# One more place for raw and one for split weights, and two query chunks interleaved between the layers of a two-layer encoder

## Chip, cores, metric

One Trainium2 chip, of which the kernel uses one core. The metric is the device time of one execution in microseconds (us); lower is better. TensorE is PE in the profile (its weight loads are PEld), VectorE is DVE, ScalarE is ACT, GpSimd is POOL, and SyncE is SP, on whose queue all transfers of weights are issued.

## The reference, cut to what matters

Two requests (256 and 512 tokens, each with 16 meta tokens in front, 800 rows in all) go through two layers. All is fp32.

```python
for i in range(2):
    mix = mla_mixer(h) if i == 0 else gqa_mixer(h)       # dense latent attention; windowed, grouped, with sinks
    h = layer_norm(ALPHA * h + mix, ln1_g[i], ln1_b[i])
    h = layer_norm(ALPHA * h + sqrelu_mlp(h, w1[i], w2[i]), ln2_g[i], ln2_b[i])

def sqrelu_mlp(x, w1, w2):                               # 1024 -> 4096 -> 1024
    h = relu(x @ w1)
    return (h * h) @ w2

def gqa_mixer(x):                                        # first steps of it
    qkv = x @ w_qkv                                      # 16 query heads, 4 key and 4 value heads of 64
    q, k = partial_rope(q), partial_rope(k)              # cos and sin on the first 16 of each 64
```

## The kernel before, in words

**Number format and weights.** Every fp32 operand of a large product is split in two fp32r parts, hi (a cast on ACT) and lo (value minus hi, on DVE), and each product is three matmuls (`mm3`, L426 to L428). A weight tile therefore passes through two places: SP loads 512 KB into a raw tile (`wraw`), ACT casts it into the hi half of a split tile (`wsp`), and DVE subtracts for the lo half (L587 and L589 in the attention parts, L1239 and L1245 in the MLP parts). There are three raw places and three split places, used in turn; a raw place is free again when both halves are made, a split place when its last matmul is done.

**Order.** Inside each of four parts (attention 0, MLP 0, attention 1, MLP 1) a `Plan` lists the tasks. PE keeps the order in which tasks are written. For ACT, DVE, POOL and SP a planner with costs per task and a number of places per kind of tile (the dictionary that begins `"wsp": 3, "wraw": 3`) chooses the order, and the program is issued in that order. Every engine then runs its own list strictly in order.

**The MLP parts.** Hidden chunks are made in pairs (`up_pair`) and multiplied down in groups of four (`down_group`), both by a scheme with 7 products instead of 8. POOL adds raw weights together first (L1258), and ACT and DVE split the sums. In a down group the seven products use weights called 1, 7, 6, 5, 3, 2, 4 in this order; products 1, 6, 5 and 3 all accumulate in the same banks X, and after each of them DVE adds the banks into `acc` (L1552) before PE may write them again. In layer 1 a product is 18 matmuls of 512 columns over three banks.

**The seam between the layers.** `attention1()` begins with the last 1/8 of layer 0's down product (`down`, 16 steps of 12 matmuls, half 0 of the tokens first; each step's bank is added to `acc` at L1803, and the sums for the mean run over POOL and DVE at L1807 and L1810 in `ssb`). Then come the second layer norm of layer 0 and the projections of layer 1. The norm of a half has three PE tasks: `mean` (a matmul with 1/1024, L603), `sums` (L618) and `scale` (L628). After `mean` DVE subtracts (L606), ACT squares (L608), DVE and POOL add squares (L612); after `scale` DVE multiplies (L633), ACT applies gain and bias (L636) and casts hi (L575), DVE makes lo (L577). The results `hb` are the right operands of the projections: query chunks `rope("q", c, half, w)` of four steps with two `hb` tiles each (6 matmuls a step), then values (four of 24 matmuls for half 0), then chunks 2 to 7. A finished query chunk is rotated by DVE (L1847, L1850), POOL (L1852) and DVE (L1855). In PE's order the norm of half 0 stands inside the down steps of half 1 (mean after step 0, sums after step 4, scale after step 6). The norm of half 1 has its mean between query chunks 0 and 1, its sums after the first step of chunk 2, its scale two steps later.

Of the kernel before, what the change touches and what calls it, by code (L numbers as in the profile page):

```python
# [12 lines left out]
F32 = mybir.dt.float32  # L13
# [341 lines left out]
def tile_encoder(ctx: ExitStack, tc: tile.TileContext, ins: dict, y):  # L355
# [64 lines left out]
        for key in [("up", j) for j in UP_FIRST[:2]] + [("dn", 7, i) for i in range(3)]:  # L420
            use(key, None, where="given")
    use(("dn", 7, 3), ins["w2c_1"][3], where="held")
    W = Weights(nc, wp, specs, 3, 3, 2)

    def mm3(out, lh, ll, rh, rl, start, stop, **kw):
        nc.tensor.matmul(out, lh, rh, start=start, stop=False, **kw)  # L426
# [64 lines left out]
    with ExitStack() as st:  # L491
        xp = pool("xp", side="right", stack=st)
        x = [xp.tile([P, 8, NT], F32R, tag=f"x{i}", name=f"x{i}") for i in range(2)]
        cos0 = xp.tile([P, NT], F32, tag="cos0", name="cos0")
        sin0 = xp.tile([P, NT], F32, tag="sin0", name="sin0")
        slices = []
        for _ in range(3):
            W.load(4)
            slices.append(W.parts)
        for k in range(8):  # L500
            xr = xp.tile([P, NT], F32, tag="xr", name=f"xr{k}", bufs=5)
            if k % 2 == 0:
                slices[0][k // 2]()
            for c in [slice(0, HALF), slice(HALF, NT)] if k < 2 else [slice(0, NT)]:
                nc.sync.dma_start(xr[:, c], ins["xT0"][k][:, c])
                split(x[0][:, k, c], x[1][:, k, c], xr[:, c])
            if k % 2 == 0:
                slices[1][k // 2]()
                slices[2][k // 2]()
        nc.sync.dma_start(gb, ins["ln_gb"])  # L510
        nc.sync.dma_start(grms, ins["rms_g"])
        nc.sync.dma_start(cos0, ins["rope0"][0])
        nc.sync.dma_start(sin0, ins["rope0"][1])
        craw = xp.tile([P, 2, NT], F32, tag="craw", name="craw")
        ss = [ssq, xp.tile([P, NT], F32, tag="ss", name="ss")]
        for o in IN_ORDER:
            w = W.get(("in", o))
            for h in range(2):
                c = slice(h * HALF, (h + 1) * HALF)
                ps = ps_w(f"in{o}{h}")  # L520
                gemm(ps[:, :HALF], w, 8, P, 0, x, (h * HALF, (h + 1) * HALF))
                pv = ps[:, :HALF]
                if o == 8:
                    sh = xp.tile([P, HALF], F32, tag="ksh", name=f"ksh{h}", bufs=2)
                    V.tensor_tensor(kr[:, h], pv, cos0[:, c], ALU.mult)
                    V.stream_shuffle(sh, pv, SWAP16)
                    V.tensor_tensor(sh, sh, sin0[:, c], ALU.mult)
                    V.tensor_tensor(kr[:, h], kr[:, h], sh, ALU.add)
                    continue
                which, first = (0, o == 0) if o < 6 else (1, o == 6)  # L530
                if o < 6:

                    g = grms[:, o : o + 1]
                    S.mul(cq[0][:, o, c], pv, g)
                    V.scalar_tensor_tensor(cq[1][:, o, c], pv, g, cq[0].bitcast(F32)[:, o, c], ALU.mult, ALU.subtract)
                else:
                    S.copy(craw[:, o - 6, c], pv)
                if first:
                    S.activation(ss[which][:, c], pv, AF.Square)
                else:  # L540
                    sq = xp.tile([P, HALF], F32, tag="sq", name=f"sq{o}{h}", bufs=2)
                    S.activation(sq, pv, AF.Square)
                    V.tensor_tensor(ss[which][:, c], ss[which][:, c], sq, ALU.add)
            if o == 7:
                for h in range(2):
                    c = slice(h * HALF, (h + 1) * HALF)
                    rs = rstd_bcast(xp, [ss[1][:, c]], HALF, 256, eps_rms, f"kv{h}")
                    for i in range(2):
                        r = craw[:, i, c]
                        V.scalar_tensor_tensor(r, r, grms[:, 6 + i : 7 + i], rs, ALU.mult, ALU.mult)  # L550
                        split(ckv[0][:, i, c], ckv[1][:, i, c], r)
# [6 lines left out]
        return [(x, y) for x in names for y in ("hi", "lo")]  # L558


    WSP = []

    def spare(given):

        return lambda k: [x for x in WSP if all(x is not y for y in given)][k]
# [1 line left out]
    def steps(plan):  # L567
# [13 lines left out]
        def weights(src, nm, tag="wsp", make=None):  # L581

            w = src.shape[-1]
            r = new("wraw", lambda: wp.tile([P, 1024], F32, tag="wraw", name=f"wraw{nm}", bufs=3))
            d = new(tag, make)
            plan.task("SP", 3.6 * w, lambda: nc.sync.dma_start(r.t[:, :w], src), writes=[r], new=[r])
            plan.task("ACT", ACT(w), lambda: S.copy(d.t[:, 0, :w], r.t[:, :w]), reads=[r], writes=[(d, "hi")], new=[d])  # L587
# [85 lines left out]

    SEQ = {0: (272, 0, 2, [(0, 272)]), 1: (528, 272, 4, [(0, 264), (264, 528)])}
    wo, l0 = ExitStack(), ExitStack()
    WSP.extend([w] + [W.get((x, 0), 0) for x in ("qr", "kv")])
    a0 = {}

    def open_output():
# [15 lines left out]

    def attention0():
        plan = Plan(
            {"wsp": 3, "wraw": 3, "w": 4, "s": 2, "qy": 2, "qsh": 2, "v0": 2, "v1": 2, "nm": 6, "rs": 6, "p": PROBS, "pt": 2, "ptm": 2, "sqa": 6, "xr": 3},
            {
                "wsp": lambda k: WSP[k],  # L700
                "w": lambda k: ps_w(f"wa_{k}"),
# [478 lines left out]
    def mlp_middle(mp, sqp, late_sum, T, n, l, tiles, yt=None):  # L1180


        plan = Plan(
            {"wsp": 3, "wraw": 3, "wx": 1, "w22": 1, "h2": 14, "sq": 6, "w": 8},
            {
                "h2": lambda k: h2_tile(mp, f"{l}_{k}", n),
                "sq": lambda k: sq_tile(sqp, f"{l}_{k}"),
# [19 lines left out]
        def raw(src, nm, tag="wraw"):  # L1207

            w = src.shape[-1]
            if tag == "wraw":  # L1210
                r = new(tag, lambda: wp.tile([P, 1024], F32, tag="wraw", name=f"wraw{nm}", bufs=3))
            else:
                r = new(tag, lambda: mp.tile([P, 1024], F32, tag=tag, name=f"{tag}{nm}", bufs=1))
            plan.task("SP", 3.6 * w, lambda: nc.sync.dma_start(r.t[:, :w], src), writes=[(r, 0), (r, 1)], new=[r])
            return r
# [552 lines left out]

    def attention1():
        plan = Plan(  # L1770
            {"wsp": 3, "wraw": 3, "wh": 1, "w": 8, "sqb": 6, "ssb": 1, "ssc": 1, "sqc": 6, "rt": 2, "sh": 1, "sma": 4, "smb": 3, "pta": 2, "ptb": 2,
             "rm": 4, "nm": 4, "rs": 4, "es": 4, "pk": 4, "ptm": 2, "mask": 1},
            {
                "wsp": spare([x for _, x in W.ready.values()]),
# [289 lines left out]
        for hf in range(2):  # L2064
            for x, t in enumerate((cos1, sin1)):
                plan.task("SP", 1400, lambda x=x, t=t, hf=hf: nc.sync.dma_start(t[hf], ins["rope1"][x][:, hf * HALF : (hf + 1) * HALF]), writes=[("rope", x, hf)])
        after0 = {0: mean0, 4: sums0, 6: scale0}
        for o in range(8):
            down(0, o)
        for o in range(8):  # L2070
            down(1, o)
            if o in after0:
                after0[o]()
        for c in range(2):
            w = wq(c)
            for i, f in enumerate(rope("q", c, 0, w)):
                f()
                if (c, i) == (0, 3):
                    mean1()
        wv = [weights(ins["w_v"][i], f"v{i}") for i in range(2)]  # L2080
        for f in values(0, wv):
            f()
        for c in range(2, 8):
            w = wq(c)
            for i, f in enumerate(rope("q", c, 0, w)):
# [256 lines left out]
```

## Time and profile before

| | us |
|---|---|
| median of 3 runs | 1798.51 (1796.97 to 1799.83) |
| the profiled execution, own time | 1798.46 |
| its span in the trace | 1796.4 |
| PE busy | 1757.5 (98%) |
| PE weight loads busy | 1626.9 (91%) |
| DVE busy | 1363.0 (76%) |
| ACT busy | 1017.1 (57%) |
| POOL busy | 639.1 (36%) |

The span is the time between the first and the last instruction that the profiler saw; the execution's own time has 2.1 us around it. A matmul's record is longer than its share of the engine, since matmuls overlap: a 384-column matmul lasts 0.34 us and the next one starts 0.175 us after it. So where PE counts as fully busy it may still be late; the distance from start to start tells. In a row of the timeline the bracket gives the idle time before the instruction and what ended it.

### The profile page before, as it was taken

What the parts mean: (1) busy time and instruction counts of PE and PEld (TensorE: products, weight loads), DVE (VectorE), ACT (ScalarE), POOL (GpSimd) and SP (SyncE); (2) the same over time, 40 slices, a digit from 0 to 9 for tenths busy, and PEclk for the clock granted to TensorE, in tenths of its full rate; (3) what the DMA queues carried; (4) which work ended last, traced back from release to release, by engine and by line L of the source; (5) the groups of instructions that cost most, each with busy time, mean ns of one, the idle gap of its engine ahead of it and who ended that gap; (6) DMA issues with size and microseconds to landing.
All of it is one profiled execution on the core that took longest, in us unless ns stands there. A gap on an engine that the chain in (4) does not pass through costs nothing.

```text
span 1796.4 us, 28830 instructions
## 1 busy us (share of the span) xinstructions
PE 1757.5 (98%) x10808; PEld 1626.9 (91%) x10808; DVE 1363.0 (76%) x2641; ACT 1017.1 (57%) x2141; POOL 639.1 (36%) x529
## 2 busy tenths in 40 slices
PE   9999999999999999999999999999999999999997
PEld 9988988889999999999999898778989888988995
DVE  5498888876876787778776777876875787778777
ACT  5377777774655445545553527775665446544652
POOL 0011111112245445545533133232244556556623
PEclk9999999999999999999999999999999999999998
DMA  5110001104311211222122121111311221222122
GB/s 198 54 36 23 27 22 38 34 29 142 113 59 47 87 58 56 83 71 71 59 94 89 51 101 48 32 40 64 114 59 47 71 71 59 83 71 71 58 84 94
DMA packets 38444, 121.70 MB, mean 68 GB/s; under 512 B 4640, under 2 KB 9376, under 8 KB 38176
## 3 DMA queue, kind: packets, MB, share of 16 engines
q1 hardware_dynamic: 38304, 119.85, 20.1%
q8 instruction: 85, 1.39, 0.3%
q14 instruction: 55, 0.45, 0.1%
HBM read 116.69 MB, written 3.15 MB: 67 GB/s over the span
## 4 chain that ended last, share of the span: by engine, by line
PE 79%; DVE 11%; ACT 4%; issue 3%; POOL 2%; DMA 1%; SPq 0%; DVEq 0%; ACTq 0%; POOLq 0%
PE w L426 14%; PE w L427 13%; PE w L428 13%; PE wb L426 4%; PE wb L427 4%; PE wb L428 4%; DVE wsp L1245 3%; PE wa L426 2%; PE wa L428 2%; PE wa L427 2%; PE wa L978 2%; DVE h L1287 2%; PE sa L426 2%; PE wb L2018 1%; PE in L427 1%
## 5 line engine op out<-in xcount | busy, mean ns | idle before, releaser
L426 PE MATMUL w<-h,wsp 128*128 128x400 f32 x632 | 218.3, 345 | 1.8 <-DVE acc L1552 1.1
L427 PE MATMUL w<-h,wsp 128*128 128x400 f32 x632 | 218.3, 345 | 0.0
L428 PE MATMUL w<-h,wsp 128*128 128x400 f32 x632 | 217.5, 344 | 0.1
L1552 DVE TENSOR_TENSOR acc<-acc,w 128x400 f32<-128x400 f32 (+1 forms) x306 | 176.8, 615 | 21.9 <-PE w L428 19.6
L1287 DVE TENSOR_TENSOR h<-sq,h 128x384 fp32r<-128x384 f32 (+1 forms) x165 | 138.0, 852 | 23.1 <-ACT h L1285 23.1
L914 POOL TENSOR_TENSOR p<-p,rs 106x512 f32<-106x512 f32 (+1 forms) x40 | 42.6, 1066 | 264.9 <-ACT pt L953 77.5
L426 PE MATMUL w<-wsp,h 128*128 128x512 f32 x300 | 119.4, 398 | 5.5 <-DVE acc L1552 5.5
L426 PEld LDWEIGHTS w<-h,wsp 128*128 128x128 f32 x632 | 118.8, 188 | 4.4 <-DVE acc L1552 3.0
L428 PEld LDWEIGHTS w<-h,wsp 128*128 128x128 f32 x632 | 118.7, 188 | 1.0 <-DVE wsp L1245 0.7
L428 PE MATMUL w<-wsp,h 128*128 128x512 f32 x300 | 119.2, 397 | 0.4
L427 PEld LDWEIGHTS w<-h,wsp 128*128 128x128 f32 x632 | 118.6, 188 | 0.9 <-DVE h L1287 0.5
L427 PE MATMUL w<-wsp,h 128*128 128x512 f32 x300 | 118.9, 396 | 0.0
L428 PE MATMUL w<-t,wsp 128*128 128x400 f32 (+1 forms) x336 | 114.5, 341 | 0.0
L427 PE MATMUL w<-t,wsp 128*128 128x400 f32 (+1 forms) x336 | 114.1, 340 | 0.0
L426 PE MATMUL w<-t,wsp 128*128 128x400 f32 (+1 forms) x336 | 114.0, 339 | 0.0
L1293 POOL TENSOR_TENSOR sq<-sq,sq 128x400 f32<-128x400 f32 (+1 forms) x56 | 75.1, 1341 | 70.2 <-DVE h L1287 61.9
L1285 ACT CAST h<-sq 128x384 fp32r<-128x384 f32 (+1 forms) x165 | 84.4, 518 | 26.1 <-POOL sq L1293 24.3
L1466 DVE TENSOR_TENSOR sq<-sq,w 128x400 f32<-128x400 f32 (+1 forms) x69 | 38.6, 560 | 60.5 <-PE w L428 60.1
L1258 POOL TENSOR_TENSOR wraw0d<-wraw0d,wraw0d 128x512 f32<-128x512 f32 x48 | 69.2, 1461 | 42.8 <-DMA wraw0d<-in_w2b_dram 29.5
L427 PE MATMUL w<-hc,wsp 128*128 128x384 f32 x232 | 78.8, 340 | 0.5 <-DVE hc L1372 0.3
L426 PE MATMUL w<-hc,wsp 128*128 128x384 f32 x232 | 79.2, 341 | 0.1
L428 PE MATMUL w<-hc,wsp 128*128 128x384 f32 x232 | 78.4, 338 | 0.0
(566 smaller groups left out, 5614.8 us busy)
## 6 DMA issues: line engine op xcount, KB each, us to landing
wrawo<-in_w_o_dram SPq DMA_DIRECT2D x32, 512.0 KB, 3.3
wraw0d<-in_w2b_dram SPq DMA_DIRECT2D x24, 512.0 KB, 3.3
wraw1d<-in_w2b_dram SPq DMA_DIRECT2D x18, 512.0 KB, 3.8
wrawq<-in_w_q_dram SPq DMA_DIRECT2D x8, 512.0 KB, 3.4
xr<-in_xT_dram SPq DMA_DIRECT2D x16, 200.0 KB, 2.7
wraw<-in_w_in_dram SPq DMA_DIRECT2D x6, 512.0 KB, 4.3
wraw<-in_w_qn_dram SPq DMA_DIRECT2D x8, 384.0 KB, 3.0
wx1d<-in_w2b_dram SPq DMA_DIRECT2D x6, 512.0 KB, 3.4
```

Of the source, the lines that this page charges most:

```text
L426: nc.tensor.matmul(out, lh, rh, start=start, stop=False, **kw)
L427: nc.tensor.matmul(out, lh, rl, start=False, stop=False, **kw)
L428: nc.tensor.matmul(out, ll, rh, start=False, stop=stop, **kw)
L914: f = lambda row=row, r=r, w=w: G.tensor_tensor(row()[:, META:T], row()[:, META:T], r().to_broadcast([qm, w]), ALU.mult)
L978: nc.tensor.matmul(av[64 * e : 64 * e + 64, :n], vt.t[:, k, h0 + 64 * e : h0 + 64 * e + 64], PT.t[:, e, k, :n], start=k == 0, stop=False, ...
L1245: lambda: V.tensor_tensor(dst.t[:, 1, dc], src.t[:, sc], dst.t.bitcast(F32)[:, 0, dc], ALU.subtract),
L1258: lambda x=x, y=y, z=z: G.tensor_tensor(x[0].t[:, x[1]], y[0].t[:, y[1]], z[0].t[:, z[1]], op),
L1285: plan.task("ACT", 530, lambda: S.copy(d.t[:, 0], c.t[:, :n]), reads=[c], writes=[(d, "hi")], new=[d])
L1287: "DVE", 570, lambda: V.tensor_tensor(d.t[:, 1], c.t[:, :n], d.t.bitcast(F32)[:, 0], ALU.subtract),
L1293: plan.task("POOL", 185 + 1.67 * n, lambda: G.tensor_tensor(out.t[:, :n], x.t[:, :n], y.t[:, :n], op), reads=[x, y], writes=[out])
L1466: plan.task("DVE", 570, lambda: V.tensor_tensor(d.t[:, :n], d.t[:, :n], ps.t[:, :n], ALU.add), reads=[ps, d], writes=[d])
L1552: f = lambda: V.tensor_tensor(z, z, ps.t[:, : z.shape[-1]], ALU.add)
```

## The change

Five edits, in one diff. (1) The numbers of raw and split places become names, `WRAW` and `NWSP`, and go from 3 to 4, in the weight loader, in the four plans and in the tile pools. (2) The list of split places that passes from the first projection to attention 0 is built from the last weights of the input projection, so that it has four. (3) The scratch that the compiler reserves for dynamic DMAs is set to 1024 where it was left at its default; that is where the room for the added places is taken. (4) At the seam, `scale` of half 0 goes from after down step 6 to after step 5. (5) Query chunks 0 and 1 are written step by step in turn, not one after the other, and `mean` of half 1 goes from between the two chunks to after the second of the four value products.

```diff
+WRAW, NWSP = 4, 4
-    W = Weights(nc, wp, specs, 3, 3, 2)
+    W = Weights(nc, wp, specs, WRAW, NWSP, NWSP - 1)
...
-            w = W.get(("in", o))
+            WSP.append(W.get(("in", o)))
+            w = WSP[-1]
...
-            r = new("wraw", lambda: wp.tile([P, 1024], F32, tag="wraw", name=f"wraw{nm}", bufs=3))
+            r = new("wraw", lambda: wp.tile([P, 1024], F32, tag="wraw", name=f"wraw{nm}", bufs=WRAW))
...
-    WSP.extend([w] + [W.get((x, 0), 0) for x in ("qr", "kv")])
+    WSP[:] = WSP[2 - NWSP :] + [W.get((x, 0), 0) for x in ("qr", "kv")]
...
-            {"wsp": 3, "wraw": 3, "wx": 1, "w22": 1, "h2": 14, "sq": 6, "w": 8},
+            {"wsp": NWSP, "wraw": WRAW, "wx": 1, "w22": 1, "h2": 14, "sq": 6, "w": 8},
...
-        after0 = {0: mean0, 4: sums0, 6: scale0}
+        after0 = {0: mean0, 4: sums0, 5: scale0}
...
-        for c in range(2):
-            w = wq(c)
-            for i, f in enumerate(rope("q", c, 0, w)):
-                f()
-                if (c, i) == (0, 3):
-                    mean1()
+        two = [rope("q", c, 0, wq(c)) for c in range(2)]
+        for f in [f for x in zip(*two) for f in x]:
+            f()
         wv = [weights(ins["w_v"][i], f"v{i}") for i in range(2)]
-        for f in values(0, wv):
+        for i, f in enumerate(values(0, wv)):
             f()
+            if i == 1:
+                mean1()
...
-    nc = bacc.Bacc("TRN2", target_bir_lowering=False, num_devices=1)
+    nc = bacc.Bacc("TRN2", target_bir_lowering=False, num_devices=1, dynamic_dma_scratch_size=1024)
```

PE's list changes at the seam alone (elsewhere only the numbers of banks differ); the planner's lists for DVE, ACT, POOL and SP change in all four parts. Lines after the diff's first places stand four lower in the changed kernel, so that L426, L589, L1245 and L1552 are L428 or L430, L593, L1249 and L1556 there. Three places are shown.

On PE, at the seam, where query chunk 0 ended before and `mean` of half 1 followed (each weight is a `wsp` number, `hb` are the normed tiles):

```order
L426 MATMUL wb_9558<-hb_9481,wsp_752 128x384
L427 MATMUL wb_9558<-hb_9482,wsp_752 128x384
L428 MATMUL wb_9558<-hb_9481,wsp_752 128x384
L603 MATMUL wb_9576<-ssb_9848,part 128x400
L426 MATMUL wb_9607<-hb_9481,wsp_687 128x384
```

and now, in the chunks' first steps (6 matmuls of one chunk, then 6 of the other):

```order
L428 MATMUL wb_9559<-hb_9481,wsp_627 128x384
L429 MATMUL wb_9559<-hb_9482,wsp_627 128x384
L430 MATMUL wb_9559<-hb_9481,wsp_627 128x384
L428 MATMUL wb_9577<-hb_9481,wsp_497 128x384
L429 MATMUL wb_9577<-hb_9482,wsp_497 128x384
L430 MATMUL wb_9577<-hb_9481,wsp_497 128x384
```

The 24 matmuls of chunk 0, the mean and the 24 of chunk 1 have become 48 in turns of six with no mean among them; the mean follows 48 value matmuls later.

On DVE, at the seam, from the first rotated query chunk to the norm of half 1, before:

```order
L1850 STREAM_SHUFFLE shq_9860<-wb_9558 128x384
L1810 TENSOR_TENSOR ssb_9848<-ssb_9848,acc 128x400 x2
L589 TENSOR_TENSOR wsp_752<-wrawv_9743,wsp_752 128x1024
L606 TENSOR_TENSOR acc<-acc,wb_9576 128x400 x6
L612 TENSOR_TENSOR sqb_9709<-sqb_9709,sqb_9673 128x400
L606 TENSOR_TENSOR acc<-acc,wb_9576 128x400 x2
L589 TENSOR_TENSOR wsp_687<-wrawq_9775,wsp_687 128x1024
L612 TENSOR_TENSOR sqb_9694<-sqb_9694,sqb_9670 128x400
L1744 TENSOR_SCALAR nsink<-sink 128x16
```

and now:

```order
L1854 STREAM_SHUFFLE shq_9890<-wb_9559 128x384
L1851 TENSOR_TENSOR rtq_9918<-wb_9577,cos_9485 128x384
L1748 TENSOR_SCALAR nsink<-sink 128x16
L1814 TENSOR_TENSOR ssb_9878<-ssb_9878,acc 128x400 x2
L593 TENSOR_TENSOR wsp_627<-wrawq_9591,wsp_627 128x1024
L1859 TENSOR_TENSOR rtq_9888<-rtq_9888,shq_9890 128x384
L593 TENSOR_TENSOR wsp_497<-wrawq_9749,wsp_497 128x1024
L610 TENSOR_TENSOR acc<-acc,wb_9628 128x400 x6
L616 TENSOR_TENSOR sqb_9715<-sqb_9715,sqb_9679 128x400
```

The instruction on the sinks and two weight splits have moved ahead of the norm; the second value weight (`wrawv`) is gone from this stretch, because it now stands among the `hb` of half 0.

On DVE, in a down group of layer 1 (`w_1`, `w_2` or `w_0`, `w_6` are the banks X; `wraw1d` are raw down weights; `h_1_` are hidden operands), before:

```order
L1287 TENSOR_TENSOR h_1_2_13184<-sq_0_12940,h_1_2_13184 128x384
L1552 TENSOR_TENSOR acc<-acc,w_1_12920 128x512
L1552 TENSOR_TENSOR acc<-acc,w_2_12956 128x512
L1245 TENSOR_TENSOR wsp_752<-wraw1d_15089,wsp_752 128x1024
L1287 TENSOR_TENSOR h_1_0_13027<-sq_0_12940,h_1_0_13027 128x384
L1552 TENSOR_TENSOR acc<-acc,w_6_13068 128x512
L1552 TENSOR_TENSOR acc<-acc,w_0_12909 128x512
L1552 TENSOR_TENSOR acc<-acc,w_4_13017 128x512
L1245 TENSOR_TENSOR wsp_622<-wraw1d_14977,wsp_622 128x1024
L1552 TENSOR_TENSOR acc<-acc,w_1_12920 128x512
```

and now:

```order
L1291 TENSOR_TENSOR h_1_2_13190<-sq_2_12963,h_1_2_13190 128x384
L1249 TENSOR_TENSOR wsp_497<-wraw1d_14963,wsp_497 128x1024
L1556 TENSOR_TENSOR acc<-acc,w_1_12920 128x512
L1556 TENSOR_TENSOR acc<-acc,w_0_12909 128x512
L1291 TENSOR_TENSOR h_1_13_13752<-sq_1_12943,h_1_13_13752 128x384
L1556 TENSOR_TENSOR acc<-acc,w_6_13073 128x512
L1556 TENSOR_TENSOR acc<-acc,w_3_13007 128x512
L1556 TENSOR_TENSOR acc<-acc,w_4_13018 128x512
L1556 TENSOR_TENSOR acc<-acc,w_1_12920 128x512
```

The split of weight 5, which stood last before the second addition from bank `w_1`, now stands before the first one, and the split of weight 6 has gone further ahead, out of this piece. On POOL the two additions of raw weights that begin a group have moved ahead of three operand additions of the first pair (L1293).

## Rows read from the trace of the kernel before

**Rows 1.** The page's first line, its busy times, and the queue that carried nearly all bytes (packets, MB, share of 16 engines).

```profile
span 1796.4 us, 28830 instructions
PE 1757.5 (98%) x10808; PEld 1626.9 (91%) x10808; DVE 1363.0 (76%) x2641; ACT 1017.1 (57%) x2141; POOL 639.1 (36%) x529
...
q1 hardware_dynamic: 38304, 119.85, 20.1%
```

**Rows 2.** Busy times by stretch: start and end, length, then PE, PEld, DVE, ACT and POOL busy (instructions), the granted PE clock, DMA share, GB/s.

```profile
900.00:950.00 50.00, 50.00 (x276) 49.81 (x275) 36.31 (x56) 29.61 (x53) 14.49 (x11) 1.00 0.32 104
950.00:1000.00 50.00, 44.84 (x236) 41.20 (x235) 36.56 (x62) 17.78 (x32) 16.74 (x13) 0.95 0.20 67
...
996.00:1000.00 4.00, 3.21 (x8) 2.55 (x9) 3.34 (x6) 0.80 (x2) 0.31 (x1) 0.50 0.28 77
1000.00:1004.00 4.00, 4.00 (x20) 3.97 (x19) 3.15 (x7) 2.08 (x5) 2.56 (x3) 0.79 0.13 54
```

**Rows 3.** PE's timeline at the seam (start, length, line, instruction, idle time before).

```profile
982.08 1.03 PE L628 MATMUL wb<-ident,rstb 100*128 100x100 f32 x8
...
984.97 0.35 PE L428 MATMUL wb<-h,wh 128*128 128x400 f32 x1
985.91 0.44 PE L426 MATMUL wb<-hb,wsp 128*128 128x384 f32 x1 [0.60 <-ACT hb L575]
...
993.57 0.33 PE L428 MATMUL wb<-hb,wsp 128*128 128x384 f32 x1
996.79 1.70 PE L603 MATMUL wb<-ssb,part 128*128 128x400 f32 x2 [2.89 <-DVE ssb L1810]
997.69 1.12 PE L426 MATMUL wb<-hb,wsp 128*128 128x384 f32 x1
...
1001.76 0.34 PE L428 MATMUL wb<-hb,wsp 128*128 128x384 f32 x1
...
1004.05 0.28 PE L426 MATMUL wb<-wsp,hb 128*16 128x256 f32 x1
...
1006.93 0.28 PE L426 MATMUL wb<-wsp,hb 128*128 128x256 f32 x1
...
1015.44 0.34 PE L426 MATMUL wb<-hb,wsp 128*128 128x384 f32 x1
...
1016.48 1.49 PE L618 MATMUL wb<-ones,sqb 128*100 128x1 f32 x16
```

**Rows 4.** DVE's timeline at the seam.

```profile
967.73 3.46 DVE L606 TENSOR_TENSOR acc<-acc,wb 128x400 f32<-128x400 f32 x7
...
972.70 2.57 DVE L612 TENSOR_TENSOR sqb<-sqb,sqb 128x400 f32<-128x400 f32 x3
...
983.52 2.48 DVE L633 TENSOR_TENSOR acc<-acc,wb 128x400 f32<-128x400 f32 x5
...
992.13 1.06 DVE L577 TENSOR_TENSOR hb<-acc,hb 128x400 fp32r<-128x400 f32 x2 [1.02 <-ACT hb L575]
...
996.66 1.21 DVE L589 TENSOR_TENSOR wsp<-wrawv,wsp 128x1024 fp32r<-128x1024 f32 x1
998.53 2.98 DVE L606 TENSOR_TENSOR acc<-acc,wb 128x400 f32<-128x400 f32 x6 [0.66 <-PE wb L603]
...
1010.38 0.17 DVE L1744 TENSOR_SCALAR nsink<-sink 128x16 f32<-128x16 f32 x1 [3.51 <-DMA sink<-in_sink_dram]
```

**Rows 5.** ACT and POOL at the seam.

```profile
984.11 1.33 ACT L636 ACTIVATE acc<-acc,gb 128x400 f32<-128x400 f32 x2 [3.15 <-DVE acc L633]
985.35 0.94 ACT L575 CAST hb<-acc 128x400 fp32r<-128x400 f32 x2
...
961.24 1.05 POOL L1810 TENSOR_TENSOR ssb<-ssb,acc 128x400 f32<-128x400 f32 x1 [1.13 <-DVE acc L1803]
...
975.89 6.14 POOL L1810 TENSOR_TENSOR ssb<-ssb,acc 128x400 f32<-128x400 f32 x4 [1.54 <-DVE acc L1803]
```

**Rows 6.** Whom PE waited for over the whole span (us in total, times, longest), and PE's timeline at one of these waits, in a down group of layer 1.

```profile
PE w L426 <- DVE acc L1552: 6.6, 10, 1.1
...
1457.72 0.40 PE L426 MATMUL w<-wsp,h 128*128 128x512 f32 x1
...
1461.91 0.40 PE L427 MATMUL w<-wsp,h 128*128 128x512 f32 x1
1462.14 0.40 PE L428 MATMUL w<-wsp,h 128*128 128x512 f32 x1
1463.42 0.47 PE L426 MATMUL w<-wsp,h 128*128 128x512 f32 x1 [0.88 <-DVE acc L1552]
```

**Rows 7.** DVE, ACT and POOL in that group.

```profile
1454.42 1.39 DVE L1552 TENSOR_TENSOR acc<-acc,w 128x512 f32<-128x512 f32 x2 [0.99 <-PE w L428]
1455.72 2.17 DVE L1245 TENSOR_TENSOR wsp<-wraw1d,wsp 128x1024 fp32r<-128x1024 f32 x1
...
1460.90 1.77 DVE L1245 TENSOR_TENSOR wsp<-wraw1d,wsp 128x1024 fp32r<-128x1024 f32 x1
1462.60 0.67 DVE L1552 TENSOR_TENSOR acc<-acc,w 128x512 f32<-128x512 f32 x1
...
1456.85 1.06 ACT L1239 CAST wsp<-wraw1d 128x1024 fp32r<-128x1024 f32 x1 [0.74 <-POOL wraw1d L1258]
...
1449.91 4.67 POOL L1258 TENSOR_TENSOR wraw1d<-wraw1d,wraw1d 128x512 f32<-128x512 f32 x3 [1.45 <-DVE wsp L1245]
```

More of the change, by code (lines that the diff above doesn't have):

```diff
@@ L471, in tile_encoder @@
         nc.tensor.matmul(warm[:, :P], part, part, start=True, stop=True)
+    WSP = []
     hp = pool("hp")
@@ L558, in both @@
         return [(x, y) for x in names for y in ("hi", "lo")]
-    WSP = []
     def spare(given):
@@ L697, in attention0 @@
         plan = Plan(
-            {"wsp": 3, "wraw": 3, "w": 4, "s": 2, "qy": 2, "qsh": 2, "v0": 2, "v1": 2, "nm": 6, "rs": 6, "p": PROBS, "pt": 2, "ptm": 2, "sqa": 6, "xr": 3},
+            {"wsp": NWSP, "wraw": WRAW, "w": 4, "s": 2, "qy": 2, "qsh": 2, "v0": 2, "v1": 2, "nm": 6, "rs": 6, "p": PROBS, "pt": 2, "ptm": 2, "sqa": 6, "xr": 3},
             {
@@ L710, in attention0 @@
         st2 = plan.stage("hidden", open_hidden)
-        wkv, wq = {0: plan.held("wsp", None, WSP[2])}, {"r0": plan.held("wsp", None, WSP[1])}
+        wkv, wq = {0: plan.held("wsp", None, WSP[-1])}, {"r0": plan.held("wsp", None, WSP[-2])}
         rows2 = [slice(0, 64), slice(64, 128)]
@@ L1210, in raw @@
             if tag == "wraw":
-                r = new(tag, lambda: wp.tile([P, 1024], F32, tag="wraw", name=f"wraw{nm}", bufs=3))
+                r = new(tag, lambda: wp.tile([P, 1024], F32, tag="wraw", name=f"wraw{nm}", bufs=WRAW))
             else:
@@ L1770, in attention1 @@
         plan = Plan(
-            {"wsp": 3, "wraw": 3, "wh": 1, "w": 8, "sqb": 6, "ssb": 1, "ssc": 1, "sqc": 6, "rt": 2, "sh": 1, "sma": 4, "smb": 3, "pta": 2, "ptb": 2,
+            {"wsp": NWSP, "wraw": WRAW, "wh": 1, "w": 8, "sqb": 6, "ssb": 1, "ssc": 1, "sqc": 6, "rt": 2, "sh": 1, "sma": 4, "smb": 3, "pta": 2, "ptb": 2,
              "rm": 4, "nm": 4, "rs": 4, "es": 4, "pk": 4, "ptm": 2, "mask": 1},
```

## Prediction

> **What bounds the kernel now.** I read the page's busy line first: PE is busy for 98% of the span, DVE for 76%, and one queue, `q1 hardware_dynamic`, carries nearly all bytes at a fifth of the DMA engines' time [rows 1]. So time can only come from PE: from its idle time, or from stretches where it counts as busy but is late. Next I read the list of waits for PE. No DMA stands near its head; its largest entry is DVE's addition into `acc` (L1552), 6.6 us in 10 waits [rows 6]. Then I went through PE's timeline for places where the distance between starts is larger than usual. One place stands out, the seam: the windows show PE busy for 44.84 of 50 us and its weight loads for 41.20, where the window before has 50.00 and 49.81, and the granted clock there averages 0.95, with 0.50 in 996 to 1000 [rows 2]. Elsewhere nothing near that size is left, so the change is worth what it takes from the seam and from the ten waits, less what it breaks.
>
> **The seam, before.** The last down matmul starts at 984.97 and fills its slot to 985.15; the sums of half 1 start at 1016.48 [rows 3]. That is 31.3 us. The work in it: 48 query matmuls at 0.175 (8.4), the mean (996.79 to 997.69, 0.9), 24 small value matmuls (1004.05 to 1006.93, 2.9), three more value blocks (1006.93 to 1015.44, 8.5) and the first step of chunk 2 (1015.44 to 1016.48, 1.0): 21.7 us. So 9.6 us are lost, in three pieces. (a) Chunk 0 takes 985.15 to 993.75 for 24 matmuls, 8.6 instead of 4.2: each pair of `hb` feeds six matmuls (1.05 us) but takes ACT 2.1 to make, by L636 (1.33 for two) and L575 (0.94 for two) in turn [rows 5]. Loss 4.4. (b) PE waits for the mean's input, DVE's L1810, until 996.79 [rows 3]: 3.0. (c) After these sparse 11 us the granted clock is 0.50, the lower of its two levels (1.2 and 2.4 GHz) [rows 2], and the first 12 matmuls of chunk 1 take 997.69 to 1001.76 from first start to last, plus a slot, instead of 2.1 [rows 3]: 2.1 with the mean.
>
> **The seam, after.** `scale` of half 0 stands one down step earlier, 12 matmuls or 2.2 us. L633, now at 983.52 behind it [rows 4], starts near 981.2, and the pairs of `hb` are ready near 984, 986, 988 and 990, plus 1.2 from the third on, because a value weight's split (1.21 in L589's row) now stands between them and DVE had 1.02 us of slack there [rows 4]. Interleaved, each pair feeds 12 matmuls, 2.1 us, which is ACT's pace. PE asks for the pairs at 985.15, 987.2, 989.3 and 991.4: no wait, and the queries end at 993.5. (a) goes whole, and with PE dense (c) goes too. The first two value tasks then run to 993.5 + 2.9 + 2.8 = 999.2, and only there PE asks for the mean. What is next late is its input: the two L1810 on DVE. Ahead of them DVE now has both chunks' rotations and the small `nsink` (0.17), which waits for a DMA: before it landed near 1010 and held DVE 3.51 [rows 4]. Its transfer stands behind a weight transfer that needs a raw place; with the fourth place that one frees when the second value weight is split, near 988, so I put the landing near 992. POOL does one `shq` ahead of its last two L1810 (1.05 each alone [rows 5]). That gives 997.2 on POOL, 998.2 with DVE's pair: in time. The mean ends near 1000.1. The norm behind it took, for half 0, from 967.73 to 972.70 + 2.57 = 975.27, so 7.5, with two other additions of half a microsecond inside [rows 4]; now 6.5 to 7.1. So the sums can start near 1007.3; PE itself is ready for them at 985.15 + 21.7 = 1006.85. I take 1007.3: **9.2 us gained** at the seam, of 9.6 at most.
>
> By PE's busy share this stretch could give back only 50 − 44.84 = 5.2 us, by its weight loads 49.81 − 41.20 = 8.6 [rows 2]. The Trainium skill ("Perfetto Trace Analysis", section "Identifying the Most-Contended Engine") says that matmul busy is no good measure because matmuls are pipelined, and to take the weight loads' busy share. With 5.2 in place of 9.6 the time below would be 4.4 later; the starts, which I use, side with the page.
>
> **The down groups of layer 1 and 0.** In the group shown, DVE makes the split of weight 5 at 1460.90 (1.77) and only then adds the bank that PE wants (1462.60); PE, which could go on at 1462.37 (the start at 1462.14 plus 0.23, the step of the two rows before), starts at 1463.42 [rows 6, 7]. That is 1.05 lost by spacing. With six such waits in layer 1 (five like this, one 1.3) I count 6.5, and by spacing 1.1 of the four smaller ones in layer 0: 7.6, against 6.6 in the list of waits, which leaves the slower restart out. In the changed order this split stands ahead of the group's first addition, where DVE now idles 0.99 before 1454.42 [rows 7]. For that its raw sum must be ready. POOL now begins it at 1449.91 and ACT casts it at 1456.85 [rows 7]. POOL's additions have moved ahead of three operand additions (about 1 us each), and the fourth raw place lets the load go earlier, so I put POOL's third sum at 1451.8, the cast at 1452.1 to 1453.2 and the split at 1453.3 to 1454.5. The first addition from X ends by 1456; PE wants that bank at 1457.72 [rows 6]. So the wait has nothing in front of it: **7.6 us gained**.
>
> **The rest.** The scratch costs nothing: weights go through SP's hardware queue, 119.85 MB on `q1`, and PE waits for no DMA [rows 1, 6]. The list of split places changes names, not work. The planner's orders for DVE, ACT, POOL and SP change in all four parts, and new short waits will come somewhere. Bound: 0 from below, with a possible gain of 0.8 at one other wait of PE on a split, to 4 from above (four waits at the largest entry's longest, 1.1 [rows 6]). I take two waits of 0.75, since four parts with 98% cover leave few: +1.5.
>
> **Sum.** 1798.46 for the profiled execution (0.05 under the median) − 9.2 − 7.6 + 1.5 = 1783.2.
>
> **Rivals.**
> 1. Only the seam gains; the group waits move to another bank of X or another weight. For it: DVE's work in a group is the same, and X takes four products in a row. Against: DVE idles 0.99 right where the split goes. 1798.46 − 9.2 + 1.5 = 1790.8.
> 2. The norm of half 1 becomes the seam's bound. POOL's L1810 took 6.14 for four, 1.54 each, where one alone took 1.05 [rows 5]; with three at 1.54, and the full 7.5 of the norm, and both on POOL and DVE at once (another 2.1), the sums come at 1011.6: gain 4.9, time 1787.5. If `nsink` still lands near 1010, it is 1010.4 + 1.8 + 0.9 + 6.5 = 1019.6, a loss of 3.1 at the seam, and 1798.46 + 3.1 − 7.6 + 1.5 = 1795.5. Against: SP is free to issue it once its place frees. In the rows DVE's split takes 2.17 and 1.77 beside POOL, 1.21 elsewhere [rows 4, 7]. The Trainium skill ("SBUF — State Buffer", section "SBUF: two separate sides") gives the cause as a shared port pair that one of DVE (with two SBUF inputs) and GpSimd holds for a whole instruction while the other is blocked; by it, more POOL work next to the norm stretches both, which is this rival.
> 3. Slower: the split of weight 5, now ahead of the first addition, blocks DVE because POOL's sum isn't earlier. With ACT's cast still at 1456.85 to 1457.91, the split ends at 1459.1 to 1460.1 and the first addition at 1459.8 or later, against 1457.72: 2.1 us in each of some 12 groups, 25.2 in all. 1783.2 + 25.2 = 1808.4. It decides from a cast that is about 2 us late on; at 1.3 us a group the gain is gone.
> 4. The replanned orders cost about what the two places give, some 15 us over four parts (fourteen waits of 1.1): 1798.5, no change to speak of. For it: DVE at 76% has little slack in the dense groups.
>
> **Chances and range.** Forecast 0.57; rival 1 0.15; rival 2 0.13 (nearly all of it at 1787.5); rival 3 0.07; rival 4 0.08. A change of 0.2% (3.6 us) is about what a measurement of this kernel can tell from none. Faster: 0.57 + 0.15 + 0.13 = 0.85; same 0.08; slower 0.07. Low end: all limits, 9.6 + 7.6 + 0.8 = 18.0, so 1780.5, less 2 for the spread of runs (1796.97 to 1799.83): 1778.5. High end: rival 1 with 4 in place of 1.5, 1793.3, so 1793; rivals 3 and 4 are left out.
>
> **What would show it.** Right: a granted clock of 1.00 from 985 to 1010; no wait of PE for L575 or L1810 at the seam; the sums of half 1 22 us after the last down matmul; no entry of PE waiting for the addition into `acc`; ACT's cast of weight 5 ahead of DVE's first addition. Wrong: DVE idle ahead of a split in each group (rival 3), a long wait of DVE at `nsink` or of PE at the sums (rival 2), new waits of PE for split weights in any part (rival 4).

## The result, and the profile after

| | before | after |
|---|---|---|
| median of 4 runs, us | 1798.61 (1796.97 to 1799.83) | 1779.89 (1779.16 to 1780.99) |
| ratio of after to before | | 0.9897, 95% interval 0.9880 to 0.9914 |
| span of the profiled execution | 1796.4 | 1778.4 |
| the profiled execution, own time | 1798.46 | 1780.31 |

The change takes 18.7 us off the median, where 15.3 were forecast. The profiled executions differ by 18.0 in span, and this is what the stretches below have to add up to. PE is busy for 9.7 us less; its weight loads hardly change [rows 1]:

```profile
span 1778.4 us, 28774 instructions
PE 1747.8 (98%) x10808; PEld 1627.4 (92%) x10808; DVE 1360.9 (77%) x2641; ACT 1012.3 (57%) x2141; POOL 632.4 (36%) x529
```

**Where it came from.** The start of the same PE instruction is read in both traces; the difference is the shift, and the growth of the shift over a stretch is what that stretch gave (negative means faster). All in us, each column from one trace against the one trace of before; the columns after the first are experiments below.

| stretch (start times of before) | after | places | seam3 | raw4 | split4 | mix |
|---|---|---|---|---|---|---|
| start to the end of attention 0 (473.03) | −1.1 | −0.9 | +0.2 | 0.0 | −1.1 | −1.3 |
| layer 0's MLP and down steps, to the last down matmul (984.97) | −0.3 | −1.2 | −1.2 | −3.1 | −2.6 | −3.1 |
| seam, to the sums of half 1 (1016.48) | −9.5 | −1.1 | −8.5 | −8.9 | −9.6 | −9.5 |
| rest of attention 1, to the first 512-column matmul (1320.90) | +0.3 | 0.0 | +0.8 | +0.8 | +0.4 | +0.3 |
| down groups of layer 1, to their last matmul (1721.32) | −8.9 | −8.9 | −0.2 | −8.5 | −5.3 | −8.0 |
| to DVE's first addition of the last product (1761.23) | +2.1 | +2.1 | 0.0 | 0.0 | +0.9 | 0.0 |
| to the end of the span (1796.40) | −0.6 | −0.6 | +0.4 | +0.3 | −0.6 | 0.0 |
| sum, before rounding | −18.0 | −10.6 | −8.5 | −19.4 | −17.9 | −21.7 |

The second row is the least certain. The traces of scratch, seam3 and seam3_sink (all below) have the orders of before in layer 0, and read −0.9, −1.2 and −0.6 there; those of places, scale6 and chunks_apart have the orders of the changed kernel, and read −1.2, −1.2 and −1.1. So both traces compared here are slow there by some 0.9 against their likes, and the change itself gave about 0.2 in layer 0, less than traces with the same orders differ by.

**The seam.** PE's timeline after (start, length, line, instruction, idle time before) at the last down matmul, the first query matmul, the first value matmul, the mean and the sums:

```profile
983.63 0.35 PE L430 MATMUL wb<-h,wh 128*128 128x400 f32 x1
983.82 0.34 PE L428 MATMUL wb<-hb,wsp 128*128 128x384 f32 x1
...
992.24 0.28 PE L428 MATMUL wb<-wsp,hb 128*16 128x256 f32 x1
...
997.82 0.83 PE L607 MATMUL wb<-ssb,part 128*128 128x400 f32 x2
...
1005.60 1.88 PE L622 MATMUL wb<-ones,sqb 128*100 128x1 f32 x16 [0.22 <-DVE sqb L616]
```

The queries follow the down steps without a gap, 48 matmuls take 8.4 us (983.82 to 992.24), the mean waits for nothing, and the sums come at 1005.60: 21.8 us after the last down matmul's slot, where before [rows 3] it was 31.3. The windows answer to [rows 2]: PE is full, its weight loads have gone from 41.20 to 48.85, and the granted clock is 1.00.

```profile
950.00:1000.00 50.00, 50.00 (x308) 48.85 (x307) 36.66 (x62) 18.90 (x34) 17.82 (x14) 1.00 0.24 77
```

On DVE (answering to [rows 4]) the second value weight is split between the `hb` tiles, `nsink` no longer waits for its transfer, and DVE waits for POOL's part of `ssb` and still ends it at 996.9, 0.9 ahead of PE's mean:

```profile
985.57 1.22 DVE L593 TENSOR_TENSOR wsp<-wrawv,wsp 128x1024 fp32r<-128x1024 f32 x1
...
992.91 0.68 DVE L1748 TENSOR_SCALAR nsink<-sink 128x16 f32<-128x16 f32 x1
...
995.73 1.18 DVE L1814 TENSOR_TENSOR ssb<-ssb,acc 128x400 f32<-128x400 f32 x2 [2.14 <-POOL ssb L1814]
```

**The groups of layer 1.** This is the group of [rows 6] and [rows 7]; PE's start after the wait at 1463.42 is now the one at 1449.98, without a wait. PE's row, then DVE's splits and its additions into `acc`:

```profile
1449.98 0.40 PE L428 MATMUL w<-wsp,h 128*128 128x512 f32 x1
...
1435.93 2.81 DVE L1249 TENSOR_TENSOR wsp<-wraw1d,wsp 128x1024 fp32r<-128x1024 f32 x2
...
1442.48 2.09 DVE L1556 TENSOR_TENSOR acc<-acc,w 128x512 f32<-128x512 f32 x3 [1.51 <-PE w L430]
...
1445.42 0.68 DVE L1556 TENSOR_TENSOR acc<-acc,w 128x512 f32<-128x512 f32 x1
1446.02 1.22 DVE L1249 TENSOR_TENSOR wsp<-wraw1d,wsp 128x1024 fp32r<-128x1024 f32 x1
1447.38 3.49 DVE L1556 TENSOR_TENSOR acc<-acc,w 128x512 f32<-128x512 f32 x5
```

Two splits now end at 1438.74, 3.7 us ahead of the first addition, and that addition waits for PE. One split stands among the additions where there were two, and it takes 1.22, not 2.17 and 1.77. What is left in the list of PE's waits for `acc` is one entry, and it is in layer 0:

```profile
PE w L428 <- DVE acc L1556: 0.8, 1, 0.8
...
PE w L428 <- ACT sq L1467: 0.7, 2, 0.5
```

**What it gave back.** In layer 0 the four old waits are gone, which by the starts had cost 1.7 us, but new ones have come that cost some 2.6 in this trace and 1.7 in that of places; the rest of the row is in pieces of under 0.3. Here are the two largest:

```profile
768.94 0.45 PE L428 MATMUL w<-h,wsp 128*128 128x400 f32 x1 [0.82 <-DVE acc L1556]
...
826.72 0.45 PE L428 MATMUL w<-h,wsp 128*128 128x400 f32 x1 [0.53 <-ACT sq L1467]
```

And in the last stretch 2.1 us are lost. The matmuls of the very last product (`dn`, L2199 before, L2203 after) are written after the four planned parts, and the compiler's scheduler places them, some between the last hidden matmuls of the MLP. Before, eight stand there (one at 1744.65, seven at 1749.11); after, seventeen, the first of them a single one, then:

```profile
1725.39 1.33 PE L2203 MATMUL dn<-wsp,h 128*128 128x512 f32 x5
...
1730.78 2.73 PE L2203 MATMUL dn<-wsp,h 128*128 128x512 f32 x11
```

Nine more at 0.235 us each are 2.1 us by which the last hidden tile comes later, and DVE's first addition with it (L2205, at 1743.84; before, L2201 at 1761.23). So the section on the change was wrong where it said that PE's list differs at the seam alone: here it differs too.

### The profile page after: what moved, and what is told of

The parts are those of the page before. It is cut to its first block, busy times and chain, and to the rows that moved or that the text cites. A ratio compares the mean times of both kernels' runs of the same rounds, so it can differ in the third digit from the quotient of the medians.

```text
span 1778.4 us, 28774 instructions
## 1 busy us (share of the span) xinstructions
PE 1747.8 (98%) x10808; PEld 1627.4 (92%) x10808; DVE 1360.9 (77%) x2641; ACT 1012.3 (57%) x2141; POOL 632.4 (36%) x529
## 4 chain that ended last, share of the span: by engine, by line
PE 86%; DVE 7%; ACT 3%; issue 3%; POOL 1%; DMA 1%; DVEq 0%; SPq 0%; ACTq 0%; POOLq 0%
PE w L429 16%; PE w L428 16%; PE w L430 16%; PE wb L428 4%; PE wb L429 4%; PE wb L430 4%; PE wa L428 3%; PE wa L430 3%; PE wa L429 2%; PE wa L982 2%; PE sa L428 2%; PE in L429 1%; PE in L428 1%; PE in L430 1%; PE wb L2022 1%
## 5 line engine op out<-in xcount | busy, mean ns | idle before, releaser
L428 PE MATMUL w<-h,wsp 128*128 128x400 f32 x632 | 217.9, 345 | 1.5 <-DVE acc L1556 0.8
L430 PE MATMUL w<-h,wsp 128*128 128x400 f32 x632 | 217.1, 343 | 0.0
L1556 DVE TENSOR_TENSOR acc<-acc,w 128x400 f32<-128x400 f32 (+1 forms) x306 | 181.9, 619 | 38.8 <-PE w L430 34.9
L1291 DVE TENSOR_TENSOR h<-sq,h 128x400 fp32r<-128x400 f32 (+1 forms) x162 | 130.1, 819 | 20.9 <-ACT h L1289 20.3
L1297 POOL TENSOR_TENSOR sq<-sq,sq 128x384 f32<-128x384 f32 (+1 forms) x65 | 84.9, 1309 | 118.2 <-DVE h L1291 101.4
L428 PEld LDWEIGHTS w<-h,wsp 128*128 128x128 f32 x632 | 118.7, 188 | 3.2 <-DVE acc L1556 1.7
L428 PE MATMUL w<-wsp,h 128*128 128x512 f32 x300 | 119.0, 397 | 0.0
L430 PEld LDWEIGHTS w<-h,wsp 128*128 128x128 f32 x632 | 118.7, 188 | 0.0
L430 PE MATMUL w<-wsp,h 128*128 128x512 f32 x300 | 118.7, 396 | 0.0
L430 PE MATMUL w<-t,wsp 128*128 128x400 f32 (+1 forms) x336 | 114.5, 341 | 0.0
L428 PE MATMUL w<-t,wsp 128*128 128x400 f32 (+1 forms) x336 | 114.0, 339 | 0.0
L1289 ACT CAST h<-sq 128x400 fp32r<-128x400 f32 (+1 forms) x162 | 82.0, 517 | 39.3 <-POOL sq L1297 38.4
L428 PE MATMUL w<-hc,wsp 128*128 128x384 f32 x232 | 79.2, 341 | 0.1
L430 PE MATMUL w<-hc,wsp 128*128 128x384 f32 x232 | 78.4, 338 | 0.0
L887 DVE TENSOR_REDUCE nm<-sa 106x1 f32<-106x528 f32 (+1 forms) x80 | 56.2, 703 | 20.5 <-PE sa L430 19.6
```

Source lines behind the costliest of these rows:

```text
L430: nc.tensor.matmul(out, ll, rh, start=False, stop=stop, **kw)
L887: plan.task("DVE", DVE(528), lambda: V.tensor_reduce(nm.t[:qm, 0:1], v(), axis=AX.XY, op=ALU.max, negate=True), reads=[ps], writes=[nm], n ...
L1289: plan.task("ACT", 530, lambda: S.copy(d.t[:, 0], c.t[:, :n]), reads=[c], writes=[(d, "hi")], new=[d])
L1291: "DVE", 570, lambda: V.tensor_tensor(d.t[:, 1], c.t[:, :n], d.t.bitcast(F32)[:, 0], ALU.subtract),
L1297: plan.task("POOL", 185 + 1.67 * n, lambda: G.tensor_tensor(out.t[:, :n], x.t[:, :n], y.t[:, :n], op), reads=[x, y], writes=[out])
L1556: f = lambda: V.tensor_tensor(z, z, ps.t[:, : z.shape[-1]], ALU.add)
```

## The experiments

All start from the changed kernel. Where a ratio is given, it is to the kernel before on the same chip; scale6, chunks_apart and seam3_sink have one time each, so their traces are read and not their times. "Lag" is the time from the slot end of the last down matmul to the sums of half 1: 31.3 before, 21.8 after.

**places: four places of each kind, the old seam**

```diff
-        after0 = {0: mean0, 4: sums0, 5: scale0}
+        after0 = {0: mean0, 4: sums0, 6: scale0}
...
+        for c in range(2):
+            w = wq(c)
+            for i, f in enumerate(rope("q", c, 0, w)):
+                f()
+                if (c, i) == (0, 3):
+                    mean1()
```

> Four raw and four split places with the old seam (scale after step 6, chunk 0, mean, chunk 1). Theory (the two gains are separate): the down groups of layer 1 lose their waits, PE's list shows no additions into acc, but the seam keeps its loss, 30 to 31.5 us from the last down matmul to the sums of half 1 with a wait of some 3 us for the mean's input; 1790 us (1788.5 to 1791.5). Rival (the places alone make the seam dense): sums 22 to 24 us after the last down matmul, 1782 us.

1788.0 us, ratio 0.9949 (0.9932 to 0.9966). The groups give 8.9 as in the changed kernel, the tail loses the same 2.1, and the seam keeps its loss, lag 30.2, with PE's old wait for the mean:

```profile
PE wb L607 <- DVE ssb L1814: 2.9, 1, 2.9
```

The two gains are separate, as the theory had it. The 1.1 us between this lag and 31.3 is not the places' doing: the control below (scratch) has 30.3 as well. Behind the mean four matmuls lasted 0.52 in both (granted clock 0.50 in 994.30 to 997.40 of places, 0.51 in 995.70 to 998.90 of scratch), nine in the trace of before (some 0.7 us more), and the first pair of `hb` came 0.35 later in that trace.

**seam3 and seam3_sink: the new seam, three places of each kind**

```diff
-WRAW, NWSP = 4, 4
+WRAW, NWSP = 3, 3
```

> The new seam with three raw and three split places. Theory: the six waits of the down groups of layer 1 stay (some 6 us in PE's list); the seam gains most of its 9.5, less a wait in the first value task, since the second value weight needs the split place of chunk 0 and can only be cast when that chunk's last matmul is done: 1.5 to 2.5 us, sums 23.5 to 24.5 us after the last down matmul; 1790.5 us (1789 to 1792.5). Rival A (the seam needs no fourth place): sums 22 us, 1789. Rival B (the sinks' transfer comes late with three raw places and holds DVE ahead of the mean's input): sums 27 us or more, 1794.

1789.9 us, ratio 0.9959 (0.9944 to 0.9974). The group waits stay. The seam's lag is 22.9, so 1.1 are missing, but not where the theory put them: no value matmul waits, and the mean does, for DVE, which waits for the sinks (rival B, though only by this much). DVE's timeline, then PE's:

```profile
998.13 0.17 DVE L1748 TENSOR_SCALAR nsink<-sink 128x16 f32<-128x16 f32 x1 [3.42 <-DMA sink<-in_sink_dram]
998.21 1.18 DVE L1814 TENSOR_TENSOR ssb<-ssb,acc 128x400 f32<-128x400 f32 x2
...
999.45 0.94 PE L607 MATMUL wb<-ssb,part 128*128 128x400 f32 x2 [1.21 <-DVE ssb L1814]
```

SP's queue shows why the transfer is late: its three weight issues from 976.98 on take 17 us, since they wait for raw places, and the sinks are issued behind them.

```profile
976.98 17.14 SPq L590 DMA_DIRECT2D wrawq<-in_w_q_dram  x3
994.17 0.42 SPq L1744 DMA_DIRECT2D mask<-in_mask_dram  x1
994.64 0.42 SPq L1747 DMA_DIRECT2D sink<-in_sink_dram  x1
```

To take the queue out of it, the sinks' load was issued on ACT's queue:

```diff
-        nc.sync.dma_start(at["sink"], ins["sink"].partition_broadcast(P))
+        nc.scalar.dma_start(at["sink"], ins["sink"].partition_broadcast(P))
```

> The new seam with three places of each kind, the load of the sinks issued on ACT's queue where it stood on SP's. Theory (with three places PE's wait for the mean's input is DVE's wait for the sinks, whose transfer stands on SP's queue behind a weight that needs a raw place): DVE's wait of 3.4 us goes, PE's wait of 1.2 with it, sums 21.8 us after the last down matmul where they were 22.9; 1.1 us less than the 1789.9 of that kernel. Rival (the split of the second value weight or POOL's sums come late by themselves): 22.9 as before.

Lag 22.2 and 1789.9 us. DVE's wait for the sinks falls from 3.42 to 0.37, but PE still waits for the mean's input, 0.55 where it was 1.21. Next late is POOL's share of the sums: the split of the second value weight (at 993.04) stands ahead of DVE's shuffle of the first query chunk (L1854), and POOL's two L1814 stand behind what POOL makes of that shuffle:

```profile
995.58 0.32 DVE L1748 TENSOR_SCALAR nsink<-sink 128x16 f32<-128x16 f32 x1 [0.37 <-DMA sink<-in_sink_dram]
998.05 1.18 DVE L1814 TENSOR_TENSOR ssb<-ssb,acc 128x400 f32<-128x400 f32 x2 [2.14 <-POOL ssb L1814]
```

So 0.7 of the 1.1 was the queue. The rest is put down to the late split by the order of these rows; no run moved that split alone. The time of this one run does not resolve 0.7.

**raw4 and split4: one more place of one kind only**

```diff
-WRAW, NWSP = 4, 4
+WRAW, NWSP = 4, 3      # raw4; split4: 3, 4
```

> The new kernel with four raw and three split places. Theory (the raw sum that is ready early is what moves the split of weight 5 ahead of the first addition): PE's waits for the additions into acc go or shrink to under 0.3 us each, the seam as with three split places (a wait of 1.5 to 2.5 in the values); 1784 us (1782 to 1786). Rival (the split place is what moves it): the six waits stay at about 1 us, 1790.

1778.9 us, ratio 0.9899 (0.9884 to 0.9914): as fast as the changed kernel with one place less. The group waits are gone (8.5), the split stands ahead of the group's first addition, as the theory said:

```profile
1437.85 2.20 DVE L1249 TENSOR_TENSOR wsp<-wraw1d,wsp 128x1024 fp32r<-128x1024 f32 x1 [1.81 <-ACT wsp L1243]
...
1442.32 2.09 DVE L1556 TENSOR_TENSOR acc<-acc,w 128x512 f32<-128x512 f32 x3 [0.23 <-PE w L430]
```

The seam has a lag of 22.5 (the sinks again, 3.02 on DVE). That it beats the forecast of 1784 is layer 0, which gives 3.1 us here and, over four traces of four of both, 0.3 to 1.2, and the tail, which loses nothing.

> The new kernel with three raw and four split places. Theory: the six waits of the down groups stay (five to seven us in PE's list), the seam is as in the new kernel, sums 22 us after the last down matmul; 1789 us (1787.5 to 1790.5). Rival (the split place is what counts): the waits are gone, 1781.

1781.3 us, ratio 0.9909 (0.9894 to 0.9923). Here the theory fell: with the raw places left at three the group waits go as well. The entry on `acc` has shrunk to one wait of 0.3, in layer 0. PE starts without a wait where it had waited, but in four of the six groups it loses some 0.56 right behind (0.2 at the sixth matmul and 0.36 at the seventh); the groups give 5.3 of the 8.9. In this kernel DVE makes three additions between the group's first split and the next one, as before:

```profile
1560.48 2.04 DVE L1249 TENSOR_TENSOR wsp<-wraw1d,wsp 128x1024 fp32r<-128x1024 f32 x1
...
1562.92 0.67 DVE L1556 TENSOR_TENSOR acc<-acc,w 128x512 f32<-128x512 f32 x1
...
1563.98 1.27 DVE L1556 TENSOR_TENSOR acc<-acc,w 128x512 f32<-128x512 f32 x2
1565.18 1.21 DVE L1249 TENSOR_TENSOR wsp<-wraw1d,wsp 128x1024 fp32r<-128x1024 f32 x1
```

The second split starts 9.0 us after PE began the group's second half (1556.18), where before it started 9.5 after (1581.51 against 1572.02) and lasted 1.78. Why PE's bank is free in time here is not shown: half a microsecond in the split's start does not explain it, and which of the planner's moves does was not followed further. The seam has its full 21.8: for the seam it is the split place that counts.

**scale6 and chunks_apart: the seam's edits one by one**

```diff
+        after0 = {0: mean0, 4: sums0, 6: scale0}                    # scale6
...
+        for c in range(2):                                          # chunks_apart
+            w = wq(c)
+            for f in rope("q", c, 0, w):
+                f()
```

> The new kernel with the scale of half 0 back after down step 6. Theory (it is worth what the first pair of normed tiles comes late): in the new kernel the pairs were ready 0.8 to 1.3 us ahead of PE; 2.2 later the first query matmul waits some 1.0 to 1.4 us, and the others follow at ACT's pace, which is PE's; sums 22.8 to 23.3 us after the last down matmul; 1781 us. Rival (it is worth nothing, the slack hides it): 21.8, 1780. Rival (the clock falls after the sparse start): 25, 1783.

Lag 22.7, so 0.9 lost, just under the range given; 1780.2 us. Only the first pair is waited for; the rest keep pace, and the clock stays at 1.00:

```profile
983.17 0.44 PE L428 MATMUL wb<-hb,wsp 128*128 128x384 f32 x1 [0.25 <-ACT hb L579]
983.78 0.45 PE L429 MATMUL wb<-hb,wsp 128*128 128x384 f32 x1 [0.17 <-DVE hb L581]
```

> The new kernel with query chunk 0 written whole ahead of chunk 1, the mean of half 1 still after the second value task. Theory (the turns of six feed PE at ACT's pace): chunk 0 waits for the pairs, which come 2.1 us apart and feed 1.05 each; with the pairs ready at the times of the new kernel chunk 1 ends 2.4 us later, sums 24.0 to 24.5 us after the last down matmul; 1782.3 us. Rival A (the mean's place alone made the gain): 22, 1780. Rival B (the clock falls to 0.5 behind chunk 0 as before): 26 to 27, 1784.5.

Lag 23.4: 1.6 us lost, less than the 2.4 expected, and no fall of the clock. The single time, 1782.7, has 2.1 us in it that came within the first 12 us of the first projection, ahead of attention 0, where nothing was changed, so it is not used. PE waits for the last two pairs:

```profile
988.61 0.44 PE L429 MATMUL wb<-hb,wsp 128*128 128x384 f32 x1 [0.68 <-DVE hb L581]
...
985.00:990.00 5.00, 4.18 (x21) 3.20 (x19) 4.93 (x9) 4.95 (x10) 0.00 (x0) 1.00 0.17 43
```

So the turns of six are worth 1.6 us and the earlier scale 0.9, each with the other in place. The rest of the 8.5 to 9.5, some 6 to 7 us, is left for the mean's place (its 3.0 us of waiting and the half clock behind it) and for what scale and turns share. The mean's place was not tried by itself, so this split of the seam's gain is not shown.

**scratch: the small scratch alone, three places, the old seam**

> The kernel before with the small scratch and the new way to build the list of split places, three raw and three split places and the old seam. Theory (the scratch costs nothing): the same time, ratio 0.998 to 1.002. Rival (a transfer or the instruction fetch uses the scratch): slower by 2 us or more.

1796.5 us, ratio 0.9992 (0.9983 to 1.0001): no difference that can be measured. The small scratch and the new list of split places cost nothing that shows.

**mix and mix_tail: the best of the parts, and the last product's order by hand**

The first edit is the mix; mix_tail has the rest too. A step (t, r, k) is three matmuls of output tile t, half r, hidden tile k; PE takes the steps in the order of the list.

```diff
-            {"wsp": NWSP, "wraw": WRAW, "wx": 1, "w22": 1, "h2": 14, "sq": 6, "w": 8},
+            {"wsp": 3, "wraw": WRAW, "wx": 1, "w22": 1, "h2": 14, "sq": 6, "w": 8},
...
+    first = [(0, 0, 0), (0, 0, 1), (0, 0, 2), (0, 1, 0), (0, 1, 1), (1, 0, 0), (1, 0, 1), (1, 0, 2), (0, 0, 3), (0, 1, 2), (0, 1, 3), (1, 0, 3)]
+    steps = first + [s for s in ((t, r, k) for t in range(6) for r in range(2) for k in range(4)) if s not in first]
...
+    with tc.manual_schedule(engines={mybir.EngineType.PE}):
```

> The new kernel in which the plans of the two MLP parts use three of the four split places, and four raw places; attention parts as in the new kernel. Theory (the parts add up): output projection and seam as with four of both, layer 0 and layer 1 groups and the tail as with four raw and three split; by the shifts of the parts 1.1 + 3.1 + 9.5 + 8.5 = 22 us under the kernel before; 1776.5 us. Rival (what differed in layer 0 was chance of one execution): 1779 to 1780.

1777.7 us, ratio 0.9894 (0.9877 to 0.9910). By the stretches the parts add up: layer 0 gives 3.1 as in raw4, so that gain is no chance of one execution, and the tail loses nothing. The profiled span is 3.7 under that of the changed kernel; the ratios' intervals overlap, so by time alone the two are not told apart.

> As the mix, and PE's order in the very last product (the last 1/8 of layer 1's down product) written by hand: the first two banks as far as they go without the last hidden tile, then finished one after the other, where the scheduler fills five banks first. Theory (the end is DVE's 31.5 us from its first addition of that product): the first addition comes 4 us earlier, and so the end; 1772.5 us. Rival (PE then waits for the last weights or hidden tile, or is itself the bound): 1775 to 1777.

1773.8 us, ratio 0.9869 (0.9854 to 0.9883), 3.9 under the mix on the same chip. DVE's first addition comes 4.0 us earlier than in the mix:

```profile
1735.59 0.69 DVE L2217 TENSOR_TENSOR acc<-acc,dn 128x512 f32<-128x512 f32 x1 [0.34 <-PE dn L2205]
...
1762.92 0.69 DVE L2217 TENSOR_TENSOR acc<-acc,dn 128x512 f32<-128x512 f32 x1 [1.10 <-PE dn L2205]
```

DVE now waits for PE at the last bank (1.10), where it did not in the mix, so PE has become a bound of the tail. No time of this kernel (1772.9 to 1774.6) reaches those of the mix (1776.7 to 1779.7) or, measured apart, of the changed kernel (1779.2 to 1781.0).

## Why the prediction was right, point by point

- **Seam: forecast 9.2, measured 9.5.** The steps held but for one cause: no wait for the pairs of `hb`, queries end at 992.24 (8.4 us after their start), the sinks' transfer in time, the mean's input 0.9 ahead, the norm 0.2 behind PE (the wait of 0.22 at the sums). On DVE that norm took 6.5 us (999.57 to 1006.03), where 6.5 to 7.1 were taken; of the two other additions read into the 7.5 of half 0 only one is there (L1803, at 972.22). Some of the 9.5 is chance in the trace of before: against the two other traces of the old seam it is 8.5. The cause that did not hold is what makes the sinks early. That their transfer stands behind a weight that needs a raw place is what SP's queue shows in seam3, but the prediction credited the fourth raw place with freeing it. raw4 has that place, and DVE still waits 3.02. split4 has three raw places, and DVE does not wait. It is the fourth split place: with it ACT casts the second value weight at 978.59 (the changed kernel) and not at 991.46 (seam3), where it waits 2.53 for PE to be done with the place; the split that follows ends at 986.79 there and at 993.76 in seam3, and SP goes on to the next issue at 987.24 and 994.17.
- **By the windows** from 950 to 1000 the seam gave 50.00 − 44.84 = 5.2 by matmul busy and 48.85 − 41.20 = 7.7 by weight loads. These windows end before the seam does. Over the seam itself PE's idle time fell by 4.9 (matmuls busy for 26.17 of 31.33 before and 21.57 of 21.79 after) and that of its weight loads by 7.6 (22.35 and 20.41), while the sums come 9.5 earlier. The Trainium skill ("Perfetto Trace Analysis", section "Identifying the Most-Contended Engine") calls matmul busy no good measure and weight loads' busy share a better one; these rows agree, and both fall short of the starts.
- **Groups: forecast 7.6, measured 9.2** (8.9 in layer 1, 0.3 in layer 0). The mechanism held for layer 1: the split has left the place between the additions. The term was mis-sized: 6.5 counted the waits that the list names, and each group but the first lost a further 0.2 to 0.4 ahead of the wait, most of it at one matmul 4.2 us ahead (0.17 to 0.26), which shows in the starts and not in the list. In layer 0 1.1 was expected and called the loss by spacing; it is the list's sum of the four waits, and by the starts they had cost 1.7. Nothing of it came through (0.3 here, and about 0.2 over four traces of each kind), because new waits took the place of the old.
- **What moves the split.** The prediction gave it to the earlier raw sum. raw4 bears that out, but split4 shows that it is not the only way: one more place of either kind is enough for most of it. Both together are not better than one: against raw4 four of both cost 1.9 to 2.9 us in layer 0 and 2.1 at the tail. Of the old group one row was misread: the three additions on POOL from 1449.91 are two for the weight cast at 1453.12 and only the third for weight 5, so its raw sum began near 1453.0 (an estimate, by thirds of the row's 4.67). The forecast did not hang on it: the splits came earlier than forecast, 3.7 ahead of the first addition.
- **Allowance: forecast +1.5 of loss, measured +0.7**, with parts that were not foreseen: −1.1 up to the end of attention 0 (one wait on a split, which was named as possible, and one at 471.85), +0.3 in the rest of attention 1, +2.1 and −0.6 in the tail. The new waits in layer 0 are counted in the groups. That these parts nearly cancel is luck: the largest, the tail's 2.1, comes from an order of PE that the prediction took to be unchanged.
- **Rivals.** Rival 1 (group waits move elsewhere) fell in layer 1 and half holds in layer 0. Rival 2's late sinks came about in seam3 and raw4, at 0.7 to 1.1 us and not 3.1. Rival 3 did not: the first addition waits for PE, not for a split. Rival 4's mechanism, replanned orders that cost, is there with some 4 to 5 us (layer 0 and tail against raw4), about a third of what it needed.

## What to carry to other kernels

Count what a stretch loses by the distance between the starts of PE's matmuls, not by its busy share or its list of waits alone; here both terms came out larger by the starts. A small load that a compute engine waits for should not stand on a queue behind large loads that wait for a place. When a planner or scheduler is given more room, compare every stretch and try each resource by itself: one more place of one kind did as well as one of both. And read a stretch in more than one trace before a cause is given for a microsecond: with the same orders layer 0 differed by up to 1.2 us here.

## What was not expected of the hardware

After the sparse stretch of the old seam the granted clock fell to its lower level (0.50 in 996 to 1000 of before [rows 2]) in all three traces of it, but for four matmuls of 0.52 us in two of them and nine in the third, with the same order on PE around it. In chunks_apart, where PE was busy for 4.18 of 5 us and waited 0.68 at most, it stayed at 1.00.
